# One core, hybrid decoder layer: queries and keys of the softmax heads turned in place by VectorE and stored as 128-byte pieces

## The chip, the cores and the metric

The kernel runs on one core of a Trainium2 chip. A core has TensorE (PE, matmuls; its weight loads are shown apart as PEld), VectorE (DVE), ScalarE (ACT), GpSimd (POOL) and SyncE (SP, which here issues nearly all DMAs). Every engine works off its own queue in order and waits for others through semaphores. The time is that of one execution on the device, in microseconds; less is better. It is given as the median of several runs.

## What is computed

One layer with 512 rows, width 2048, all in float32: a combined projection, gated linear attention (4 heads, "gla"), eight softmax heads of width 128 with normed queries and keys and a relative bias, an output projection, and a gated feed-forward part. For the softmax heads:

```python
h = rms_norm(x, norm1_g[l])
proj = h @ w_in[l]
qa, ka, va, ra, ga, qb, kb, vb = jnp.split(proj, split_points, axis=-1)
...
qb = rms_norm(qb.reshape(Bsz, S, DIL_HEADS, DIL_DH), q_norm_g[l])
kb = rms_norm(kb.reshape(Bsz, S, DIL_HEADS, DIL_DH), k_norm_g[l])
out_b = dilated_mixer(qb, kb, vb.reshape(Bsz, S, DIL_HEADS, DIL_DH), rel_bias)
mix = jnp.concatenate([out_a.astype(x.dtype), out_b.astype(x.dtype)], axis=-1)
x = x + mix @ w_out[l]
h2 = rms_norm(x, norm2_g[l])
x = x + (jax.nn.silu(h2 @ w_gate[l]) * (h2 @ w_up[l])) @ w_down[l]
```

In `dilated_mixer` the scores are `q · k / sqrt(128)` plus a bias; the norm weights `q_norm_g` and `k_norm_g` are vectors over the 128 features of a head, so in a score they act as a product of both, feature by feature. With 512 rows the three dilated branches reduce to a causal softmax with a bias table over the distance.

## The kernel before

**The large products** follow a scheme of seven products in place of eight (a Strassen variant). A `Pair` works on two blocks of 512 weight columns. The seven products run in the order P1, P5, P6, P3, P7, P2, P4, each over four groups of 512 rows of the weights (for the input projection). One *item* is a product with a group: its weights are a quarter (`wa`, `wb`, `wc`, `wd`, 512 KB, loaded on SP at L259) or a sum of quarters, made by DVE at L298 (P5, P6, P7 and P4 need one; P5's is `wa<-wb`). The item's weights are split in two parts for precision: `wh`, a cast on ACT (L376), and `wl`, the remainder on DVE (L380). PE then runs 8 matmuls with `wh` and 4 with `wl` (L405). There are two buffers each for `wh` and `wl`, so casts and splits run one or two items ahead of PE.

When a product closes a part of an output, ACT (L324) evicts the accumulators to `seed` tiles, DVE adds further products to them (L343), or ACT evicts into `cout` (L638, the last part); then `final` inside `final_proj` (L1072 ff.) is called with two finished tiles of 128 rows by 512 columns. For the blocks `qb0`, `kb0`, `qb1`, `kb1` (each holds four heads) `heads_norm` norms every head: squares on ACT (L1055), small steps on both engines (L178 to L183), and the scaling on DVE (L1060). Then L1086 stores the tile as rows of 2 KB to a DRAM array `proj[name]` of 512 rows by 512 columns.

**The pairs** run in this order: the gla queries and keys, `va1`/`va0`, `qb0`/`kb0`, `vb1`/`vb0`, `qb1`/`kb1`, the gate pair, two pairs of the output projection, eleven of the feed-forward part, and its down projection. A pair's last part, `cout`, is finished while the next pair begins.

**The background** is a list of generators, stepped between the items of a pair. `gla_head` pairs (L831 to L930) make the gla heads: products with constant matrices `mats` (L849, L850, L865), DVE steps L869 to L882, products L889 to L920, and squares of the result `oT` (L924), its scaling (L927) and its store (L930). `dil_heads(h)` runs two softmax heads side by side: loads of `q`, `k`, `v` and a bias tile (L959 to L963), 16 transposes on PE with 4 evictions on ACT that put the norm weight on each (L970, L971), then for blocks of 128 rows the scores (L979), logits and sums (L982 to L989), transposes of the probabilities (L996) and products with the values (L1003). Heads 0 to 3 start after `vb0` is finished, heads 4 to 7 after `qb1` is finished, beside the gate pair.

**What sets the order.** The first pair has a script; elsewhere a list scheduler lays each engine's queue from the program and its own costs. On SP each DMA also waits for the eighth DMA before it.

The lane names in the rows below: lane 0 of a head pair uses tiles `q`, `k`, `v`, `T`, `L`, `oT`; lane 1 uses `qT`, `kT`, `r`, `PT`.

Of the kernel before, what the change touches and what calls it, by code (L numbers as in the profile page):

```python
# [13 lines left out]
AF = mybir.ActivationFunctionType  # L14
ALU = mybir.AluOpType
# [3 lines left out]
P = 128  # L19
# [112 lines left out]
def block_kernel(ctx: ExitStack, tc: tile.TileContext, ins, out):  # L132
    nc = tc.nc
# [18 lines left out]
    def nm(s):  # L152
        uid[0] += 1
        return f"{s}_{uid[0]}"

    def dram(shape, name):
        return dr.tile(shape, F32, name=name, tag=name)

    def bank():
        return ps.tile([P, 512], F32, name=nm("bank"), tag="bank")  # L160

    def work(tag, shape=(P, 512), bufs=1):
        return mp.tile(list(shape), F32, name=nm(tag), tag=tag, bufs=bufs)

    def const(shape, name):
        return cp.tile(list(shape), F32, name=name, tag=name)
# [3 lines left out]
    load = nc.sync.dma_start  # L170
    store = nc.sync.dma_start

    mats = const([P, 4, P], "mats")
    ident, tri, stri, causal = (mats[:, i, :] for i in range(4))
# [95 lines left out]
    def halves(t):  # L270
        return t.rearrange("p (b a) -> p b a", b=2)
# [157 lines left out]
    def first_pair(op, rows, w1, w2, final, begin):  # L429
# [24 lines left out]
        def fetch(name, g):  # L454
            if name[0] == "r" and name != "row":
                b, h = 2 * g + (name[2] == "2"), int(name[1] == "2")
                load(raw[b, h], ins["xt"][b, h])
            elif name == "gw":
                load(kinds[:, :2].rearrange("p a g j n -> p (a g j) n"), ins["gw"])
            elif name == "sm":  # L460
                small_loads()
            else:
                q[name[0], g] = load_quarter(rows, name[0], g, w1 if name[0] in "ac" else w2)
# [169 lines left out]
    def emitted(c, scale):  # L633

        res = []
        for m in range(2):
            t = cpool.tile([P, 512], F32, name=nm("cout"), tag="C")
            nc.scalar.activation(halves(t), unfolded(c[m]), AF.Copy, scale=scale(m))  # L638
            res.append(t)
        return res  # L640
# [4 lines left out]
    gq = const([P, 1], "gq")  # L645
    gk = const([P, 1], "gk")
# [14 lines left out]
    def small_loads():  # L661
        load(mats, ins["mats"])
        load(g2, ins["g2"])
        
        load(gq, ins["q_norm_g"].rearrange("(p o) -> p o", o=1))
        load(gk, ins["k_norm_g"].rearrange("(p o) -> p o", o=1))
        nc.gpsimd.tensor_scalar(gq, gq, 1.0 / math.sqrt(128.0), None, op0=ALU.mult)
        load(gb, bass.AP(tensor=ins["gla_onorm_g"].tensor, offset=0, ap=[[0, P], [1, DV]]))

    def bias_tables():  # L670
# [49 lines left out]
    for g in range(4):  # L720
        for b in (2 * g, 2 * g + 1):
            if g < 2:
                t = apool.tile([P, 2, 512], F32, name=nm("xT"), tag="A")
# [56 lines left out]
    def gates():  # L780
# [28 lines left out]
        for t in range(4):  # L809
# [15 lines left out]
    proj = {n: dram([S, 512], n) for n in  # L825
            ("qa", "ka", "va0", "va1", "qb0", "kb0", "vb0", "vb1", "qb1", "kb1")}
# [3 lines left out]
    def head_cols(src, h, w=P):  # L830
        return src.rearrange("(t p) c -> p t c", p=P)[:, :, h * w : (h + 1) * w]  # L831
# [109 lines left out]
    def dil_head(h, lane):  # L941


        s = h // 4

        def tile_(name):
            if lane == 0:
                return work("oT" if name == "o" else name)
            if name in "qk":
                return work(name + "T")  # L950
            return rpool.tile([P, 512], F32, name=nm("r"), tag="r")

        def logits(b):
            if lane == 0:
                return work("L", bufs=2)
            return tile_("L") if b % 2 else work("PT")

        qh, kh, vh = tile_("q"), tile_("k"), tile_("v").rearrange("p (t d) -> p t d", t=4)
        load(qh.rearrange("p (t d) -> p t d", t=4), head_cols(proj[f"qb{s}"], h % 4))  # L959
        load(kh.rearrange("p (t d) -> p t d", t=4), head_cols(proj[f"kb{s}"], h % 4))  # L960
        load(vh, head_cols(proj[f"vb{s}"], h % 4))
        tb = tile_("T")
        load(tb, bass.AP(  # L963
            tensor=rep_d.tensor, offset=h * P * NB + P - 1, ap=[[NB - 1, P], [1, 512]]
        ))
        yield
        for src, g in ((qh, gq), (kh, gk)):
            tp = bank()
            for t in range(4):
                nc.tensor.transpose(tp[:, t * P : (t + 1) * P], src[:, t * P : (t + 1) * P], ident)  # L970
            nc.scalar.activation(src, tp, AF.Copy, scale=g)  # L971
        yield
        ot = tile_("o")
        lgs = {}

        def scores(b):
            n = P * (b + 1)
            lp = bank()
            nc.tensor.matmul(lp[:, :n], qh[:, b * P : (b + 1) * P], kh[:, :n], start=True, stop=True)  # L979
            lg = lgs[b] = logits(b)  # L980
            st = work("mx", (P, 4), bufs=4)
            recent["head"] = nc.vector.tensor_tensor_reduce(  # L982
                lg[:, :n], lp[:, :n], tb[:, 512 - n :], -1.0, 3.0e38, ALU.add, ALU.min, st[:, 0:1]
            ).ins
            nc.scalar.activation(
                lg[:, :n], lg[:, :n], AF.Exp, scale=-1.0, bias=st[:, 0:1], accum_out=st[:, 2:3]
            )
            nc.vector.reciprocal(st[:, 3:4], st[:, 2:3])
            recent["head"] = nc.vector.tensor_scalar(  # L989
                lg[:, :n], lg[:, :n], st[:, 3:4], None, op0=ALU.mult  # L990
            ).ins

        def turn(b, tp):
            n = P * (b + 1)
            for k in range(b + 1):
                nc.tensor.transpose(  # L996
                    tp[:, k * P : (k + 1) * P], lgs[b][:, k * P : (k + 1) * P], ident
                )
            nc.scalar.copy(lgs[b][:, :n], tp[:, :n])

        def values(b, op):
            for k in range(b + 1):
                nc.tensor.matmul(  # L1003
                    op, vh[:, k, :], lgs[b][:, k * P : (k + 1) * P], start=(k == 0), stop=(k == b)
                )

        for i in range(6):
            tp = bank() if 1 <= i <= 4 else None
            if i >= 2:
                op = tp[:, i * P : (i + 1) * P] if i < 4 else bank()[:, :P]  # L1010
                values(i - 2, op)
            if tp is not None:
                turn(i - 1, tp)
            if i >= 2:
                nc.scalar.copy(ot[:, (i - 2) * P : (i - 1) * P], op)
            if i < 4:
                scores(i)
            if i == 5:
                store(mix_d[4 + h // 2][:, :, h % 2, :].rearrange("b p n -> p b n"), halves(ot))
            yield  # L1020

    def dil_heads(h):

        lanes = [dil_head(h, 0), dil_head(h + 1, 1)]
        for _ in range(8):
            for lane in lanes:
                next(lane)
            if _ == 7:
                done.update((id(mix_d[4 + h // 2]), half) for half in range(2))
            yield  # L1030
# [17 lines left out]
    def heads_norm(tiles):  # L1048

        ss = work("ss", (P, 8), bufs=4)  # L1050
        jk = work("jk", (P, P // 2)).bitcast(mybir.dt.bfloat16)
        by_head = [t.rearrange("p (h d) -> p h d", h=4) for t in tiles]
        for m in range(2):
            for h in range(4):
                nc.scalar.activation(  # L1055
                    jk, by_head[m][:, h, :], AF.Square, accum_out=ss[:, 4 * m + h : 4 * m + h + 1]
                )
        rsqrt_mean(ss, P)
        for m in range(2):
            nc.vector.tensor_tensor(  # L1060
                by_head[m], by_head[m],
                ss[:, 4 * m : 4 * m + 4].unsqueeze(2).to_broadcast([P, 4, P]), op=ALU.mult,
            )
# [12 lines left out]
    def final_proj(n1, n2):  # L1076
        def final(half, which, tiles, acc_):
            if tiles is None:
                tiles = emitted(acc_, lambda m: row_scale(half, m))
            name = (n1, n2)[which]  # L1080
            dst = proj[name]
            if name[:2] in ("qb", "kb"):
                heads_norm(tiles)
            for m in range(2):
                r = half * 256 + m * P
                store(dst[r : r + P, :], tiles[m])  # L1086
            if half == 1 and name in ready:
                background.extend(ready[name]())

        return final  # L1090
# [521 lines left out]
```

## Time and profile before

| | |
|---|---|
| median of three runs | 1911.92 us (1911.07 to 1914.44) |
| span of the profiled execution | 1915.3 us |
| TensorE clock granted | 1.000 of full speed |
| PE busy | 1897.7 us, 99% |
| DVE busy | 1674.1 us, 87% |
| ACT busy | 1069.7 us, 56% |
| POOL busy | 12.9 us, 1% |

The profile shows one execution. Its span is from the first to the last instruction, and it is a little above the three runs that were timed. A row of the timeline reads: start, duration, engine, line, operation, output<-input, shape and count, and in brackets the idle time before it with what ended it. A row of a group gives busy time and the mean of one instruction, then the idle time of the engine just before such instructions. In a row of one source line the three durations are minimum, median and maximum in ns. TensorE takes a float32 product with one 128-row stationary operand in several passes or one, so the count in a timeline row can be twice that of the program.

### The profile page before, as it was taken

The page shows a single profiled execution, that of the slowest core. Times are in us where ns is not written, and L with a number is a line of the kernel's source. Part 1 is how long each engine was busy: PE and PEld are TensorE (multiplying, and loading weights), DVE is VectorE, ACT ScalarE, POOL GpSimd, SP SyncE. Part 2 cuts the span into 40 slices and gives each one's busy share as a digit, 9 for nine tenths or more (in the row PEclk, how much of TensorE's full clock was granted, in tenths as well). Part 3 has the DMA queues.
Part 4 walks back from the last instruction along what each step waited for, and adds up shares of the span by engine and source line. Part 5 has one row for each costly group of instructions (what it writes and reads, how often), then busy time and mean ns, then how long its engine had stood idle before and what let it go on. Part 6 is the DMA issues. An engine that isn't in the chain of part 4 may idle for free.

```text
span 1915.3 us, 25304 instructions
## 1 busy us (share of the span) xinstructions
PE 1897.7 (99%) x9002; PEld 1644.2 (86%) x9002; DVE 1674.1 (87%) x1956; ACT 1069.7 (56%) x1567; POOL 12.9 (1%) x22
## 2 busy tenths in 40 slices
PE   9999999999999999999999999999999999999999
PEld 7888888888888788888888888888888888878887
DVE  8898797778899999888888888888889979989987
ACT  8654564667776665544544544544456546536443
POOL 0000010000000000000000000000000000000000
PEclk9999999999999999999999999999999999999999
DMA  9636456444537464465465465465466675785662
GB/s 341 211 111 247 153 162 186 139 159 149 188 121 236 154 215 125 123 182 177 130 188 176 121 193 159 125 197 156 129 198 217 196 245 173 257 280 178 239 220 66
DMA packets 246806, 345.73 MB, mean 181 GB/s; under 512 B 107718, under 2 KB 154607, under 8 KB 246680
## 3 DMA queue, kind: packets, MB, share of 16 engines
q1 hardware_dynamic: 246392, 343.99, 56.5%
q8 instruction: 70, 1.15, 0.3%
q14 instruction: 56, 0.46, 0.1%
q10 hardware_dynamic: 288, 0.14, 0.0%
HBM read 286.10 MB, written 60.31 MB: 181 GB/s over the span
## 4 chain that ended last, share of the span: by engine, by line
PE 81%; DVE 5%; DMA 4%; issue 2%; ACT 1%; SPq 0%; DVEq 0%; ACTq 0%
PE acc L405 77%; DVE wl L380 2%; PE bank L1003 1%; PE bank L979 1%; DVE wa L298 1%; PE bank L996 0%; DVE AS L199 0%; DMA xn_d<-PT 0%; DMA xn_d<-oT 0%; ACT wh L376 0%; DMA wc<-in_w_down 0%; PE bank L918 0%; DMA wb<-in_w_out 0%; DMA kT<-turned_d 0%; DMA k<-y_d 0%
## 5 line engine op out<-in xcount | busy, mean ns | idle before, releaser
L405 PE MATMUL acc<-wh,AS 128*128 128x512 f32 x3008 | 711.0, 379 | 1.2 <-ACT wh L376 1.2
L405 PEld LDWEIGHTS acc<-wh,AS 128*128 128x128 f32 x3008 | 568.1, 189 | 83.0 <-ACT wh L376 2.5
L376 ACT CAST wh<-wa 128x1024 fp32r<-128x1024 f32 x376 | 394.3, 1049 | 402.4 <-PE acc L405 372.6
L405 PE MATMUL acc<-wh,AA 128*128 128x512 f32 x2256 | 533.5, 379 | 0.1
L380 DVE TENSOR_TENSOR wl<-wa,wh 128x1024 fp32r<-128x1024 f32 x376 | 456.5, 1215 | 61.3 <-ACT wh L376 49.9
L405 PEld LDWEIGHTS acc<-wh,AA 128*128 128x128 f32 x2256 | 426.1, 189 | 60.9 <-ACT wh L376 0.5
L405 PE MATMUL acc<-wl,AS 128*128 128x512 f32 x1504 | 394.0, 384 | 6.9 <-DVE wl L380 6.7
L405 PEld LDWEIGHTS acc<-wl,AS 128*128 128x128 f32 x1504 | 280.7, 189 | 56.4 <-DVE wl L380 15.8
L405 PE MATMUL acc<-wl,AA 128*128 128x512 f32 x1128 | 294.9, 384 | 0.2
L405 PEld LDWEIGHTS acc<-wl,AA 128*128 128x128 f32 x1128 | 211.2, 189 | 33.9 <-DVE wl L380 3.2
L376 ACT CAST wh<-wb 128x1024 fp32r<-128x1024 f32 x94 | 98.6, 1049 | 122.9 <-PE acc L405 113.2
L376 ACT CAST wh<-wc 128x1024 fp32r<-128x1024 f32 x94 | 98.6, 1049 | 119.3 <-PE acc L405 99.7
L376 ACT CAST wh<-wd 128x1024 fp32r<-128x1024 f32 x94 | 98.5, 1048 | 91.3 <-PE acc L405 74.0
L298 DVE TENSOR_TENSOR wa<-wc,wa 128x1024 f32<-128x1024 f32 x94 | 114.1, 1218 | 30.8 <-DMA wc<-in_w_gate 19.5
L380 DVE TENSOR_TENSOR wl<-wd,wh 128x1024 fp32r<-128x1024 f32 x94 | 114.2, 1218 | 30.2 <-ACT wh L376 26.9
L380 DVE TENSOR_TENSOR wl<-wc,wh 128x1024 fp32r<-128x1024 f32 x94 | 114.4, 1217 | 28.0 <-ACT wh L376 27.4
L380 DVE TENSOR_TENSOR wl<-wb,wh 128x1024 fp32r<-128x1024 f32 x94 | 114.2, 1215 | 9.0 <-ACT wh L376 7.3
L298 DVE TENSOR_TENSOR wb<-wd,wb 128x1024 f32<-128x1024 f32 x94 | 114.0, 1215 | 0.4
L298 DVE TENSOR_TENSOR wa<-wb,wa 128x1024 f32<-128x1024 f32 x94 | 113.6, 1210 | 0.8
L298 DVE TENSOR_TENSOR wa<-wd,wa 128x1024 f32<-128x1024 f32 x94 | 112.9, 1215 | 0.1
L343 DVE SCALAR_TENSOR_TENSOR seed<-acc,rs,seed 128x512 f32<-128x512 f32 x96 | 70.3, 744 | 15.3 <-PE acc L405 14.1
L324 ACT ACTIVATE seed<-acc,rs 128x512 f32<-128x512 f32 x96 | 60.7, 681 | 5.1 <-PE acc L405 5.1
(317 smaller groups left out, 1263.0 us busy)
## 6 DMA issues: line engine op xcount, KB each, us to landing
wa<-in_w_gate SPq DMA_DIRECT2D x44, 512.0 KB, 3.4
wb<-in_w_up SPq DMA_DIRECT2D x44, 512.0 KB, 5.8
wd<-in_w_up SPq DMA_DIRECT2D x44, 512.0 KB, 4.2
wc<-in_w_gate SPq DMA_DIRECT2D x44, 512.0 KB, 3.4
wa<-in_w_in SPq DMA_DIRECT2D x24, 512.0 KB, 5.1
wc<-in_w_in SPq DMA_DIRECT2D x24, 512.0 KB, 3.6
wb<-in_w_in SPq DMA_DIRECT2D x24, 512.0 KB, 5.4
wd<-in_w_in SPq DMA_DIRECT2D x24, 512.0 KB, 5.1
```

Source lines behind the costliest of these rows:

```text
L298: nc.vector.tensor_tensor(src, other, src, op=ALU.subtract)
L324: nc.scalar.activation(halves(t), unfolded(src[m]), AF.Copy, scale=self.scale(half, m))
L343: nc.vector.scalar_tensor_tensor(halves(seed[m]), unfolded(src[m]), self.scale(half, m), halves(seed[m]), op0=ALU.mult, op1=ALU.add,)
L376: nc.scalar.copy(high[k], sources[k])
L380: recent["low"] = nc.vector.tensor_tensor(low[k], sources.pop(k), high[k].bitcast(F32), op=ALU.subtract).ins
L405: nc.tensor.matmul(p.dst[prod][m], a[:, jj, hl, m * P : (m + 1) * P], folded(w[i][:, jj, :]), start=fresh and g == 0 and i == 0 and jj == ...
L979: nc.tensor.matmul(lp[:, :n], qh[:, b * P : (b + 1) * P], kh[:, :n], start=True, stop=True)
L1003: nc.tensor.matmul(op, vh[:, k, :], lgs[b][:, k * P : (k + 1) * P], start=(k == 0), stop=(k == b))
```

## The change

Four things change, and the rest of the program is the same text.

1. Each finished tile of `qb*` and `kb*` (128 rows, 512 columns) is transposed in place by DVE. That operation turns each block of 32 by 32 by itself: partition `32a + i`, column `32c + n` receives what stood in partition `32a + n`, column `32c + i`.
2. The turned tile is stored by four DMAs, one for each 32 partitions: each writes 32 × 16 pieces of 32 numbers (128 bytes), so that `proj[name]` now holds features as rows and tokens as columns. There are 64 such stores of 64 KB in place of 16 of 256 KB.
3. The loads of `q` and `k` for a head become 128 whole rows of 2 KB, already turned. The 16 transposes of each head pair on PE (64 in all) go, as do their 16 evictions on ACT.
4. The norm weight of the queries, already divided by sqrt(128), is multiplied once with that of the keys on POOL. One ACT operation per head puts this product on the queries (8 in all); the keys are used as loaded.

```diff
@@ small_loads
         nc.gpsimd.tensor_scalar(gq, gq, 1.0 / math.sqrt(128.0), None, op0=ALU.mult)
+        nc.gpsimd.tensor_tensor(gq, gq, gk, op=ALU.mult)
@@ dil_head
-        load(qh.rearrange("p (t d) -> p t d", t=4), head_cols(proj[f"qb{s}"], h % 4))
-        load(kh.rearrange("p (t d) -> p t d", t=4), head_cols(proj[f"kb{s}"], h % 4))
+        load(qh, proj[f"qb{s}"][h % 4 * P : h % 4 * P + P, :])
+        load(kh, proj[f"kb{s}"][h % 4 * P : h % 4 * P + P, :])
...
-        for src, g in ((qh, gq), (kh, gk)):
-            tp = bank()
-            for t in range(4):
-                nc.tensor.transpose(tp[:, t * P : (t + 1) * P], src[:, t * P : (t + 1) * P], ident)
-            nc.scalar.activation(src, tp, AF.Copy, scale=g)
+        nc.scalar.activation(qh, qh, AF.Copy, scale=gq)
@@ final_proj
-            if name[:2] in ("qb", "kb"):
+            turned = name[:2] in ("qb", "kb")
+            if turned:
                 heads_norm(tiles)
             for m in range(2):
                 r = half * 256 + m * P
-                store(dst[r : r + P, :], tiles[m])
+                if not turned:
+                    store(dst[r : r + P, :], tiles[m])
+                    continue
+                nc.vector.transpose(tiles[m], tiles[m])
+                for a in range(4):
+                    store(
+                        dst.rearrange("(c i) t -> i c t", i=32)[:, :, r + 32 * a : r + 32 * a + 32],
+                        tiles[m][32 * a : 32 * a + 32, :].rearrange("i (c n) -> i c n", n=32),
+                    )
```

In the changed program the lines behind these edits have other numbers: the scaling of the heads is L1057 (before L1060), the transposes L1087, the stores L1089 (before L1086), the scale of the queries L968, the scores L976 (before L979), the transposes of the probabilities L993 (before L996) and the products with the values L1000 (before L1003); the lines of gla are one higher.

The scheduler orders the queues anew. The first place is the start of the pair `vb1`/`vb0`, while `qb0`'s last part, `cout`, is finished. On DVE before, the sums for P5 (`wa<-wb`) stand between the splits; this piece holds those of its second and third group (`wa_2537`, `wa_2577`), and the scaling of `cout` (L1060) follows five rows on:

```order
L298 TENSOR_TENSOR wa_2537<-wb_2668,wa_2537 128x1024
L380 TENSOR_TENSOR wl_2622<-wa_2577,wh_2618 128x1024
L181 SCALAR_TENSOR_TENSOR so_2550<-so_2550,rt_2558 128x2
L298 TENSOR_TENSOR wb_2668<-wd_2785,wb_2668 128x1024
L182 TENSOR_TENSOR so_2550<-so_2550,rt_2558 128x2
L298 TENSOR_TENSOR wa_2577<-wb_2705,wa_2577 128x1024
L183 SCALAR_TENSOR_TENSOR so_2550<-so_2550,rt_2558 128x2
L178 TENSOR_SCALAR ss_2593<-ss_2593 128x8
L380 TENSOR_TENSOR wl_2652<-wa_2620,wh_2647 128x1024
```

On DVE at this place now (`cout_2614` and `cout_2616` are the two tiles, `oT_2576` the gla result, and `wa_2562<-wb_2701` is the sum of P5's second group):

```order
L928 SCALAR_TENSOR_TENSOR oT_2576<-bank_2574,so_2575,gb 128x256 x2
L1057 TENSOR_TENSOR cout_2614<-cout_2614,ss_2618 128x512
L1057 TENSOR_TENSOR cout_2616<-cout_2616,ss_2618 128x512
L1087 STREAM_TRANSPOSE cout_2614<-cout_2614 128x512
L1087 STREAM_TRANSPOSE cout_2616<-cout_2616 128x512
L870 SCALAR_TENSOR_TENSOR qT_2784<-bank_2774,L_2721 128x4x64
L298 TENSOR_TENSOR wa_2562<-wb_2701,wa_2562 128x1024
```

The sum that P5's second group needs has moved behind the scaling and the transposes of `cout`, and behind a gla step.

On PE at the same place before, P5's second group (`wh_2703`, `wl_2708`) runs around the gla products L865, and its third (`wh_2724`) follows at once:

```order
L405 MATMUL acc_2701<-wh_2703,AS_77_529 128x512 x2
L405 MATMUL acc_2702<-wh_2703,AS_77_529 128x512 x2
L865 MATMUL bank_2741<-mats,q_2637 128x128 x4
L865 MATMUL bank_2742<-mats,k_2639 128x128 x4
L405 MATMUL acc_2701<-wl_2708,AS_77_529 128x512
L405 MATMUL acc_2702<-wl_2708,AS_77_529 128x512
L405 MATMUL acc_2701<-wl_2708,AS_77_529 128x512
L405 MATMUL acc_2702<-wl_2708,AS_77_529 128x512
L405 MATMUL acc_2701<-wh_2724,AS_81_549 128x512 x2
```

On PE now, from the end of P5's second group (`wl_2741`) to its third (`wh_2757`):

```order
L405 MATMUL acc_2735<-wl_2741,AS_77_530 128x512
L890 MATMUL bank_2833<-qT_2784,kT_2788 64x128
L890 MATMUL bank_2833<-L_2721,kT_2788 64x128
...
L902 MATMUL bank_2846<-v_2674,k_2672 128x256 x2
L919 MATMUL bank_2895<-v_2674,PT_2831 128x256 x2
L921 MATMUL bank_2895<-st_2849,qT_2784 128x256
L405 MATMUL acc_2734<-wh_2757,AS_81_550 128x512 x2
```

The whole gla step, to its result `bank_2895`, now stands between two items. On DVE and ACT that result's squares, scaling and the sum for `wh_2757` follow it in this order: on DVE `L928 ... oT_2897`, then `L298 ... wa_2602`, whose cast is `wh_2757`.

The second place is the start of the gate pair, where heads 4 and 5 begin. On PE before, their transposes stand within the last P5 item (`wh_4337`, `wl_4342`), and the next item follows:

```order
L405 MATMUL acc_4278<-wh_4337,AS_56_388 128x512 x2
L970 MATMUL bank_4371<-mats,q_4296 128x128 x4
L970 MATMUL bank_4377<-mats,k_4297 128x128 x4
L970 MATMUL bank_4383<-mats,qT_4304 128x128 x4
L970 MATMUL bank_4389<-mats,kT_4305 128x128 x4
L405 MATMUL acc_4277<-wl_4342,AS_56_388 128x512
```

On PE now, from the end of P5's third group (`wl_4342`) to its fourth (`wh_4358`):

```order
L405 MATMUL acc_4299<-wl_4342,AS_81_550 128x512
L976 MATMUL bank_4437<-k_4318,q_4317 128x128
L976 MATMUL bank_4446<-kT_4326,qT_4325 128x128
L993 MATMUL bank_4476<-mats,L_4439 128x128
L976 MATMUL bank_4479<-k_4318,q_4317 128x256
L993 MATMUL bank_4487<-mats,PT_4448 128x128
L976 MATMUL bank_4490<-kT_4326,qT_4325 128x256
L1000 MATMUL bank_4514<-L_4439,v_4319 128x128
L976 MATMUL bank_4520<-k_4318,q_4317 128x384
L1000 MATMUL bank_4528<-PT_4448,r_4327 128x128
L976 MATMUL bank_4534<-kT_4326,qT_4325 128x384
L405 MATMUL acc_4298<-wh_4358,AS_56_389 128x512 x2
```

Ten products of the heads stand in a row between two items, where before the first scores came two items after the transposes. On SP, at the same place, the eight stores of `cout` stand directly ahead of the loads of `k`, `v`, the bias and `q`. On DVE the sum for `wh_4358` stands behind the first two rounds of both heads:

```order
L985 RECIPROCAL mx_4449<-mx_4449 128x1
L986 TENSOR_SCALAR PT_4448<-PT_4448,mx_4449 128x128
L298 TENSOR_TENSOR wa_4244<-wb_4339,wa_4244 128x1024
L985 RECIPROCAL mx_4482<-mx_4482 128x1
L979 ISA r_4492,mx_4493<-bank_4490,r_4331 128x256
```

Before, that sum (`wa<-wb` of the fourth group) came before the heads' first scores.

## The prediction

> **What bounds the kernel now.** I read the page from the top (busy shares, then the chain that ended last) and then what TensorE waits for.
>
> ```profile
> span 1915.3 us, 25304 instructions
> PE 1897.7 (99%) x9002; PEld 1644.2 (86%) x9002; DVE 1674.1 (87%) x1956; ACT 1069.7 (56%) x1567; POOL 12.9 (1%) x22
> PE 81%; DVE 5%; DMA 4%; issue 2%; ACT 1%; SPq 0%; DVEq 0%; ACTq 0%
> L405 PE MATMUL acc<-wl,AS 128*128 128x512 f32 x1504 | 394.0, 384 | 6.9 <-DVE wl L380 6.7
> ```
>
> PE is busy for 99% of the span and its largest wait, for the split `wl`, is 6.7 us in all. So a PE instruction that goes is worth its time, and a new wait of PE costs its length unless matmuls stand in front of it. VectorE at 87% is close behind, and in the stretch where the change hits first it is full:
>
> ```profile
> 258.00:292.00 34.00, 34.00 (x176) 29.29 (x175) 33.42 (x55) 20.60 (x51) 8.05 (x3) 1.00 0.35 109
> ```
>
> The columns after the stretch's length are PE, weight loads, DVE, ACT and POOL busy: DVE 33.42 of 34.00 us.
>
> **What goes from PE.** The chain of waits holds the removed transposes (L970) as whole pieces; three of the four:
>
> ```profile
> 334.23 1.75 PE bank L970 x16
> 388.39 1.75 PE bank L970 x16
> 463.45 1.75 PE bank L970 x16
> ```
>
> Sixteen take 1.75 us, and there are four groups (64 fewer matmuls on PE): 4 × 1.75 = **−7.0 us**. The Trainium skill, VectorE: DVE Perf Modes, section The three transpose paths, has 390 ns for one 128x128 transpose on TensorE (bf16): by that the removal would be worth 64 × 0.39 = 25.0 us, an estimate from that page, and the whole change would save about 6. The trace differs, as 1.75 / 16 is 0.109 us in a pipelined row, so its value stands.
>
> **What is added off PE.** Sixteen in-place DVE transposes; no such instruction is in the trace in place, but the same shape between two tiles is:
>
> ```profile
> L1396 DVE STREAM_TRANSPOSE oT<-seed x22: 700/704/711, 770.7 to 1511.0; 128x512 f32<-128x512 f32 x22
> L1086 SPq DMA_DIRECT2D qb<-cout x4: 319/320/320, 278.4 to 456.9; - x4
> DMA to landing us min/median/max: 2.0/2.3/5.8
> L1398 SPq DMA_DIRECT2D turned_d<-PT x88: 302/504/1530, 775.1 to 1518.3; - x88
> L1398 SPq DMA_DIRECT2D turned_d<-oT x88: 302/488/1785, 771.5 to 1513.2; - x88
> DMA to landing us min/median/max: 1.7/2.2/5.0
> ```
>
> I take 0.70 us each, 11.2 in all; 0.68 and the 1.23 of a 1024-wide operation bound it. Twelve of the sixteen I cost at nothing: they stand beside long rows of matmuls whose sums are ahead. Without that cover the same twelve would cost 8.4. The stores go from 16 of 2 KB rows to 64 of 512 pieces of 128 bytes. The nearest rows are L1398's, 64 KB also in many short pieces: 0.49 us to issue, 2.2 to land, against 0.32 and 2.3 of a row store (L1086). So four stores hold SP for 1.96 us instead of 0.32. The loads of q and k become contiguous; the strided ones land in 3.5 (below), and between 2.1 and 5.0, the fastest and slowest loads of that size, I keep 3.5. ACT loses 16 evictions of about 0.68 us and gains 8 scales that I price the same: 5.4 us less work on an engine that is not the bound. The one product on POOL, at the start, is hidden by 12.9 us busy in 1915.
>
> **Place A, the start of the pair after qb0/kb0 (264 to 290 us).** In the order of the change, ACT's cast for P5's second group and the DVE sum before it stand behind the whole finishing of `cout`, and the gla steps are bunched on PE. Rows of before that price it:
>
> ```profile
> 276.87 1.26 ACT L324 ACTIVATE seed<-acc,rs 128x512 f32<-128x512 f32 x2
> 265.45 0.39 ACT L924 ACTIVATE oT<-bank 128x256 f32<-128x256 f32 x1 [0.17 <-DMA ong_d<-oT]
> 266.08 0.20 ACT L924 ACTIVATION_READ_ACCUMULATOR oT<-bank 128x1 f32 x1
> 259.04 0.17 DVE L178 TENSOR_SCALAR ss<-ss 128x8 f32<-128x8 f32 x1
> 260.32 1.29 DVE L1060 TENSOR_TENSOR seed<-seed,ss 128x512 f32<-128x512 f32 x2
> 261.54 0.87 DVE L927 SCALAR_TENSOR_TENSOR oT<-bank,so,gb 128x256 f32<-128x256 f32 x2
> 283.38 0.41 DVE L869 SCALAR_TENSOR_TENSOR qT<-bank,L 128x256 f32<-128x256 f32 x1
> 263.57 1.23 DVE L298 TENSOR_TENSOR wa<-wb,wa 128x1024 f32<-128x1024 f32 x1
> 262.22 1.05 ACT L376 CAST wh<-wa 128x1024 fp32r<-128x1024 f32 x1 [1.49 <-PE acc L405]
> 274.10 1.05 PE L849 MATMUL bank<-mats,T 128*128 128x128 f32 x8
> 275.45 1.43 PE L405 MATMUL acc<-wl,AA 128*128 128x512 f32 x4
> 276.72 1.89 PE L405 MATMUL acc<-wh,AS 128*128 128x512 f32 x8
> 279.31 1.89 PE L405 MATMUL acc<-wh,AS 128*128 128x512 f32 x8
> 281.04 0.60 PE L865 MATMUL bank<-mats,q 128*128 128x128 f32 x4
> 281.83 1.11 PE L405 MATMUL acc<-wl,AS 128*128 128x512 f32 x4
> ```
>
> From the end of P1 on PE: evictions 1.26; squares of `oT` 0.83 (265.45 to 266.28); the norm's small steps 1.28 (259.04 to 260.32); `cout` scaled and `oT` written 2.09 (260.32 to 262.41); two transposes 1.40; L869 0.41; the sum 1.23; the cast 1.05. That is 9.55, with 0.3 for handovers 9.85. In front of P5's second group PE has one item (276.72 to 279.31, 2.59), the eight-and-two small ones (274.10 to 275.45, 1.35) and L865 (281.04 to 281.83, 0.8): 4.75. PE waits 9.85 − 4.75 = **5.1**.
>
> Then P5's third group: PE runs the gla outputs (L921 of the change) and has nothing after them until squares 0.83, small steps 1.28, `oT` 0.87, sum 1.23, cast 1.05 and 0.3 of handovers are done: **5.6**. Place A costs 10.7. In before the same sums stood between the splits, one or two items early, and no row above shows PE idle.
>
> The loads behind the eight stores on SP:
>
> ```profile
> wb<-in_w_in SPq DMA_DIRECT2D x24, 512.0 KB, 5.4
> ```
>
> P1 ends at 275.45 + 1.43 = 276.88, both tiles are turned 6.86 later at 283.7 (the five terms up to the transposes), the first at 283.0; eight issues of 0.49 end at 287, and `wb` lands at 292.8. The sum that reads it comes at 276.88 + 9.85 + 2.59 (an item) + 2.2 (gla products, an estimate) + 2.98 (squares, steps, `oT`) = 294.5. So SP hides it by 1.7 us; if the issues took 0.7 it would not. At the kb groups too SP is held 3.3 us longer (8 × 0.49 − 2 × 0.32) ahead of weight loads that are issued several items early; I price this at nothing, at most 3.3 a group.
>
> **Place B, the gate pair's first heads (453 to 480 us).** The change lays the scores of heads 4 and 5 on PE straight behind P5's third group and ahead of its fourth, whose sum is also behind two rounds of the heads on DVE. Rows:
>
> ```profile
> 454.39 1.22 DVE L298 TENSOR_TENSOR wa<-wd,wa 128x1024 f32<-128x1024 f32 x1
> 455.52 1.28 DVE L1060 TENSOR_TENSOR cout<-cout,ss 128x512 f32<-128x512 f32 x2
> q<-qb SPq DMA_DIRECT2D x4, 256.0 KB, 3.5
> 464.45 0.68 ACT L971 ACTIVATE q<-bank,gq 128x512 f32<-128x512 f32 x1
> 458.97 1.89 PE L405 MATMUL acc<-wh,AS 128*128 128x512 f32 x8
> 461.56 1.89 PE L405 MATMUL acc<-wh,AS 128*128 128x512 f32 x8
> 470.21 0.38 PE L979 MATMUL bank<-k,q 128*128 128x128 f32 x2
> 470.44 0.39 PE L979 MATMUL bank<-kT,qT 128*128 128x128 f32 x2
> 473.33 0.28 DVE L989 TENSOR_SCALAR PT<-PT,mx 128x128 f32<-128x128 f32 x1
> ```
>
> The sum at 454.39 that stood ahead of L1060 stands earlier now, so the norm can start at 454.4 and the first tile is turned by 454.4 + 1.28 + 0.70 = 456.4. Eight stores of 0.49 end at 460.3, the last lands 2.2 later at 462.5, q's load (0.4 to issue, 3.5 to land) at 466.4, the scale ends 0.68 later: 467.1. The third group ends at 461.56, 0.3 later as its neighbour's split waits for the transposes: 461.9. PE waits **5.2**, and 0.3 more for the split. From the first scores to the second head's scaled logits before took 3.4 (470.21 to 473.61); then sum 1.22, cast 1.05, 0.3: 6.0. In that time PE has ten small products: scores of 128, 256 and 384 columns for two heads at 0.23 a 128 columns (470.21 to 470.44), 2 × 6 × 0.23 = 2.8, and four of 128 columns at half that or more, 0.5: an estimate of 3.3, so it waits **2.7**. Place B costs 8.2.
>
> **Sum:** −7.0 + 10.7 + 8.2 = +11.9. The profiled span would go from 1915.3 to 1927; that execution is just above the three runs (1911.07 to 1914.44), so I carry the difference to their median 1911.92 and forecast **1924 us**. From 560 us on the two orders agree; between 500 and 560 some rows change places, for which I allow 2 us either way.
>
> **The rivals.**
> 1. *The covers hold* (faster). If PE's queue reaches both places late enough, or the handovers are shorter, that the sums come in time, only the removal is left: 1911.9 − 7.0 = 1904.9. It needs PE to be over 10 us behind ACT at the two places; ACT's evictions wait for the end of PE's own P1, which speaks against it. It decides only where place A and B together cost under 3. Chance 0.07.
> 2. *One place waits*: with A alone 1911.9 − 7.0 + 10.7 = 1915.6, with B alone 1913.1. For it: B's first half falls to 3.8 if q lands in 2.1. Against it: both waits are made by the order of a queue, which no duration undoes. Chance 0.12.
> 3. *The short pieces are slow.* If each store of place B took 1.785 to issue and 5.0 to land, the worst of L1398, q would come 8 × 1.30 + 2.8 = 13 us later: 1937. For it: pieces of 128 bytes, 512 of them in 64 KB; against it: medians of 0.49 and 2.2. Chance 0.14. The Trainium skill, DMA: Bandwidth & Descriptors, section Specifications, wants at least 512 bytes per transfer for line rate and says that below it data is read, modified and written; that speaks for this rival, and L1398's median shows none of it, but its landing is of 64 KB only.
>
> My forecast has 0.67, with a range of its own of 1916 to 1932: unknown prices (in-place transpose 0.68 to 1.23, load 2.1 to 5.0, the region after 500) move it by some 8 either way. The range of 8 in 10 takes in one-place cases and the lower half of the slow stores: 1912 to 1935. A measurement tells about 0.2%, 3.8 us: under 1908.1 is faster (rival 1, 0.07), within it are the one-place cases and a little of the forecast's edge (0.12), above 1915.7 the rest, 0.81.
>
> **What would show it.** L970 gone and PE's matmuls 64 fewer; a wait of L405 for ACT's `wh` of about 5 us twice near 275 to 290; PE's scores (L976 of the change) waiting for ACT's q near 462, then L405 for `wh` again; store issues of L1089 at 0.5 us. If these waits are under 1 us each I am wrong about the order deciding; if the stores take over 1 us to issue, rival 3 holds; if waits stand past 560 us, something I did not see moved.

## The result and the profile after

| | before | changed |
|---|---|---|
| median of the timed runs | 1913.18 us (1911.07 to 1917.69, 4 runs) | 1935.86 us (1934.73 to 1936.59, 4 runs) |
| span of the profiled execution | 1915.3 us | 1934.8 us |
| clock granted to PE, mean | 1.000 | 0.993 |

The ratio is 1.0116 with a 95% interval of 1.0105 to 1.0128; the medians lie 22.7 us apart. The forecast was 1924 us with a range up to 1935, so the direction was right, the forecast loss was about half of the measured one, and the time lies 0.9 us outside the range.

The head of the page of the changed kernel, and its list of what PE waited for (total, times, longest):

```profile
span 1934.8 us, 25201 instructions
PE 1902.5 (98%) x8938; PEld 1645.0 (85%) x8938; DVE 1684.0 (87%) x1972; ACT 1066.5 (55%) x1559; POOL 6.7 (0%) x23
...
PE acc L405 <- ACT wh L376: 9.3, 2, 5.4
PE bank L976 <- ACT q L968: 5.3, 1, 5.3
PE acc L405 <- DVE wl L380: 4.8, 9, 0.9
PE bank L993 <- DVE L L986: 2.0, 2, 1.5
PE bank L1105 <- DVE seed L1153: 2.0, 1, 2.0
```

The reader is to see that PE is *busier* than before (1902.5 against 1897.7 us) with 64 matmuls fewer, although the waits that were forecast are there too. Both waits for the cast `wh` stand at place A, that for the scaled `q` at place B. That matmuls took longer shows in the clock that PE was granted. These are stretches of the changed kernel (the columns behind the length are the busy times of PE, weight loads, DVE, ACT and POOL, then PE's clock, the busy share of the DMA engines and GB/s); before, the clock was 1.00 in all four:

```profile
280.00:300.00 20.00, 10.71 (x49) 7.62 (x48) 13.33 (x28) 5.14 (x12) 1.25 (x2) 0.77 0.73 229
300.00:320.00 20.00, 20.00 (x83) 17.18 (x84) 17.60 (x16) 9.12 (x14) 0.00 (x0) 0.89 0.15 49
460.00:480.00 20.00, 14.65 (x67) 12.21 (x66) 10.41 (x15) 7.80 (x18) 0.00 (x0) 0.96 0.44 117
480.00:500.00 20.00, 18.41 (x70) 14.36 (x71) 15.85 (x31) 11.19 (x22) 0.00 (x0) 0.78 0.59 227
```

And PE's own rows at place A (start, duration):

```profile
278.28 1.03 PE L405 MATMUL acc<-wl,AS 128*128 128x512 f32 x4
...
285.72 3.78 PE L405 MATMUL acc<-wh,AS 128*128 128x512 f32 x8 [3.92 <-ACT wh L376]
289.29 1.80 PE L405 MATMUL acc<-wl,AS 128*128 128x512 f32 x4
...
299.84 0.80 PE L405 MATMUL acc<-wh,AS 128*128 128x512 f32 x1 [5.37 <-ACT wh L376]
```

Eight products with `wh` that took 1.89 us before take 3.78: behind each wait PE ran at half clock, and the item after the first wait lasted 5.3 us (285.72 to 291.02) instead of 2.6. (The last row is the first matmul of its item; all eight took 3.78 us here too.)

At place B the chain runs along SP, and the first scores, which took 0.38 us before, take 0.80:

```profile
468.99 4.17 SPq L1089 DMA_DIRECT2D qb<-cout  x8
474.92 0.33 SPq L960 DMA_DIRECT2D q<-qb  x1
478.97 0.72 ACT L968 ACTIVATE q<-q,gq 128x512 f32<-128x512 f32 x1 [9.80 <-DMA q<-qb]
479.74 0.80 PE L976 MATMUL bank<-k,q 128*128 128x128 f32 x2 [5.34 <-ACT q L968]
478.60:488.80 10.20, 7.47 (x19) 4.80 (x20) 6.22 (x17) 5.99 (x14) 0.00 (x0) 0.50 1.04 399
```

The load of `q` stands behind the eight stores and lands 4.0 us after its issue. The last row is a stretch: for these 10.2 us the clock was 0.50, and PE was busy for 7.5 of them.

**Where the time came from.** PE runs the same 659 items (P1 to P4 of all pairs but the first) in the same sequence in all kernels here, so the start of an item can be compared. The table gives how much later it starts than in the first profile of before:

| kernel (profile) | item 54 (258 us before) | 66 (297) | 95 (387) | 128 (498) | 147 (566) | last (1910) |
|---|---|---|---|---|---|---|
| the change | 0.8 | 16.1 | 14.3 | 21.9 | 24.8 | 19.5 |
| e6, before again | 1.4 | 1.4 | 1.4 | 1.4 | 1.0 | -1.4 |
| e1, row stores | 0.4 | 0.4 | -1.3 | -3.5 | -1.9 | -7.2 |
| e2, pieces only | 1.3 | 12.6 | 10.9 | 19.9 | 22.3 | 16.8 |
| e3, waits filled | 1.0 | 11.5 | 11.7 | 19.1 | 21.2 | 16.3 |
| e5, SP and ACT | 2.5 | 2.5 | 3.9 | 3.1 | 5.5 | 0.8 |
| e7, bare removal | 0.1 | 0.1 | -1.7 | -3.5 | -0.7 | -3.3 |
| e9, bare, heads 0 to 3 | 1.7 | 1.7 | 1.0 | -0.8 | 0.0 | -4.8 |
| e10, bare, heads 4 to 7 | 0.0 | 0.0 | 0.0 | -0.3 | 5.0 | 0.4 |
| e11, heads 0 to 3, SP and ACT | 0.7 | 0.7 | 0.3 | -1.5 | -1.1 | -6.8 |
| e12, heads 0 to 3, SP | 0.4 | 16.1 | 14.9 | 13.1 | 15.0 | 10.1 |
| e13, heads 4 to 7, SP | 0.3 | 0.3 | 0.3 | 9.4 | 9.6 | 3.9 |
| e14, e12 with its waits filled | -0.3 | 10.2 | 12.8 | 12.1 | 11.8 | 6.3 |

For the change: place A costs 16.1 − 0.8 = 15.3 us, the two groups of transposes at 334 and 388 us bring 1.8 each (item 128 is behind both), place B costs 21.9 − (16.1 − 3.5) + 1.75 = 11.1 with the third group, and between 498 and 566 us another 2.9 + 1.75 = 4.7 come although the fourth group is gone. Behind 566 us the first profile of before is itself slow by some waits that its second profile has less of (−2.4 there), so the last column is read with 2 to 3 us of doubt, and the times decide.

### The profile page after: what moved, and what is told of

Read it like the earlier page. It is cut to its first block, busy times and chain, and to the rows that moved or that the text cites. A ratio compares the mean times of both kernels' runs of the same rounds, so it can differ in the third digit from the quotient of the medians.

```text
span 1934.8 us, 25201 instructions
## 1 busy us (share of the span) xinstructions
PE 1902.5 (98%) x8938; PEld 1645.0 (85%) x8938; DVE 1684.0 (87%) x1972; ACT 1066.5 (55%) x1559; POOL 6.7 (0%) x23
## 4 chain that ended last, share of the span: by engine, by line
PE 81%; DVE 6%; DMA 3%; issue 2%; ACT 1%; SPq 0%; DVEq 0%; ACTq 0%
PE acc L405 76%; DVE wl L380 2%; DVE wa L298 1%; PE bank L1000 1%; PE bank L976 1%; DVE AS L199 1%; DMA top<-mix_d 0%; PE bank L993 0%; PE bank L1105 0%; ACT wh L376 0%; DMA mix_d<-r 0%; PE bank L919 0%; DMA qT<-S_d 0%; DMA wc<-in_w_down 0%; PE bank L902 0%
## 5 line engine op out<-in xcount | busy, mean ns | idle before, releaser
L405 PEld LDWEIGHTS acc<-wh,AS 128*128 128x128 f32 x3008 | 570.4, 190 | 92.7 <-ACT wh L376 11.1
L298 DVE TENSOR_TENSOR wa<-wc,wa 128x1024 f32<-128x1024 f32 x94 | 114.5, 1221 | 30.9 <-DMA wc<-in_w_gate 20.5
L298 DVE TENSOR_TENSOR wb<-wd,wb 128x1024 f32<-128x1024 f32 x94 | 114.1, 1218 | 0.4
L298 DVE TENSOR_TENSOR wa<-wb,wa 128x1024 f32<-128x1024 f32 x94 | 113.5, 1210 | 0.8
L298 DVE TENSOR_TENSOR wa<-wd,wa 128x1024 f32<-128x1024 f32 x94 | 112.9, 1216 | 0.1
L343 DVE SCALAR_TENSOR_TENSOR seed<-acc,rs,seed 128x512 f32<-128x512 f32 x96 | 70.3, 744 | 14.3 <-PE acc L405 14.2
```

The source lines that it names most:

```text
L298: nc.vector.tensor_tensor(src, other, src, op=ALU.subtract)
L343: nc.vector.scalar_tensor_tensor(halves(seed[m]), unfolded(src[m]), self.scale(half, m), halves(seed[m]), op0=ALU.mult, op1=ALU.add,)
L405: nc.tensor.matmul(p.dst[prod][m], a[:, jj, hl, m * P : (m + 1) * P], folded(w[i][:, jj, :]), start=fresh and g == 0 and i == 0 and jj == ...
```

## The experiments

In all of them the median of before was 1912.3 to 1913.8 us, run beside them on the same chip. Where the heads read a wrong arrangement, the expectation says so.

**e1 and e2: the stores or the transposes?** e1 keeps VectorE's transposes and stores rows; e2 keeps the pieces and drops the transposes.

```diff
 e1
-                for a in range(4):
-                    store(dst.rearrange(...)[...], tiles[m][32 * a : 32 * a + 32, :]...)
+                store(dst[r : r + P, :], tiles[m])
 e2
-                nc.vector.transpose(tiles[m], tiles[m])
```

> The change, but each turned tile is stored by one DMA of 2 KB rows in place of four of 128-byte pieces (the heads then read queries and keys in a wrong arrangement, the work of every engine but the DMA pieces is that of the change). Theory, that the loss is the queue order which the many small stores brought about, and the halved clock behind the waits: the queues stand as before at both places, so only the 64 transposes go from PE: about 1913 - 7 = 1906 us, no PE wait over 2 us, clock 1.000. Rival, that VectorE's 16 transposes in a full stretch make the sums late: above 1920, with waits of PE for the cast at 280 to 300 us as in the change.

Measured: 1910.29 us, ratio 0.9984 (0.9975 to 0.9994), clock 1.0.

> The change without the 16 transposes on VectorE (blocks are stored unturned, so the heads read other numbers), with the 64 stores of 128-byte pieces. Theory: the stores bring the order, so it stays slow: 1925 to 1940, with one or two waits of PE of over 4 us near 280 to 300 us and half clock behind each. Rival, that the transposes on VectorE cost the time: about 1906, as PE has lost its transposes and VectorE has gained none.

Measured: 1932.13 us, ratio 1.0097 (1.0082 to 1.0112). What PE waited for, first e1, then e2:

```profile
PE acc L405 <- DVE wl L380: 5.6, 8, 1.9
PE bank L993 <- DVE L L986: 3.1, 2, 2.3
```

```profile
PE acc L405 <- ACT wh L376: 12.0, 3, 6.1
PE acc L405 <- DVE wl L380: 4.4, 6, 1.5
PE bank L993 <- DVE L L986: 4.1, 2, 2.2
```

The waits for the cast come with the pieces on SP and go with them; VectorE's 16 transposes alone make none. In e1 PE's queue at both places is that of before, in e2 the gla steps are bunched too. So the loss hangs on the 64 small stores on SP and the queue order that comes with them. At place A the chain to the late cast holds no DMA, so there it is the order; at place B the eight issues on SP are themselves in the chain, and e1 shortens them as well as it changes the order, so the two are not told apart there. And e1 saved 2.5 us, not the 7 of its expectation.

**e3: fill the waits at place A.** Ten products into a bank that nobody reads: four behind L866 and, in the piece below, six behind L921 of that head.

```diff
+            if h == 3 and ts == (0, 1):
+                wb_ = bank()
+                for _ in range(6):
+                    with tc.issue_after(last):
+                        nc.tensor.matmul(wb_, ident, mats.rearrange("p a n -> p (a n)"), start=True, stop=True)
```

> The change with ten products of no use laid on PE inside the two waits at 282 and 295 us (four of 0.86 us and six, into a bank that nobody reads); all other queues in the same order. Theory, that the waits cost once as idle time and once more as half clock behind them: the idle time stays, filled, and the half clock goes: 5.1/2 + 4.7/2 = 4.9 us less than the change, about 1931, and the granted clock after 284 and 298 us is 1.0. Rival, that the half clock costs nothing because PE waits for others then anyway: within 1 us of the change, 1935 to 1937.

Measured: 1936.08 us, ratio 1.0117 (1.0102 to 1.0132): no gain in the times. In its profile the clock behind the waits was full,

```profile
286.00:288.00 2.00, 2.00 (x10) 1.76 (x11) 1.78 (x3) 0.00 (x0) 0.00 (x0) 1.00 0.70 120
300.00:302.00 2.00, 2.00 (x11) 1.75 (x10) 2.00 (x2) 0.89 (x1) 0.00 (x0) 1.00 0.02 9
```

and the item behind them started 4.6 us earlier than in the change, but PE then waited 1.7 us for a cast at 321 us. Inconclusive as to the time; e12 and e14 repeat it with place A alone.

**e4 and e5: the whole change, its stores on other queues.** In e4 POOL issues those of `kb0`, `kb1` and `qb0`, and SP and ACT in turn those of `qb1`; in e5 SP and ACT in turn issue all.

```diff
 e4
+                    q = nc.gpsimd if name != "qb1" else (nc.sync, nc.scalar)[a % 2]
 e5
+                    q = (nc.sync, nc.scalar)[a % 2]
-                    store(
+                    q.dma_start(
```

> The whole change, but the stores of kb0, kb1 and qb0 are issued by POOL and those of qb1 by SP and ACT in turn; with this PE's queue stands as before at both places. Theory: 1913 - 7 = 1906 us, up to 1909 if ACT's four issues of about 0.5 us delay a cast; clock 1.000. Rival, that pieces of 128 bytes themselves are too slow for the heads' loads or for the weight loads beside them: 1916 or more, with PE waiting for the scale of q or for a weight sum.

Measured: 1955.65 us, ratio 1.0222 (1.0205 to 1.0239). Far slower, and by neither mechanism. POOL's timeline:

```profile
289.50 0.66 POOL L1090 DMA_DIRECT2D qb<-seed  x1 [1.80 <-issue]
291.96 0.65 POOL L1090 DMA_DIRECT2D qb<-seed  x1 [1.80 <-issue]
294.41 0.66 POOL L1090 DMA_DIRECT2D qb<-seed  x1 [1.80 <-issue]
```

POOL put out one such store every 2.45 us, against 0.50 on SP, so eight took 20 us; gla's small steps on POOL stood behind them (PE waited 11.1 us for one), and later the loads of `k` and what SP held behind those (15.6 us for a cast).

> The whole change, but the stores of 128-byte pieces are issued by SP and ACT in turn, half each, and none by POOL. PE's queue stands nearly as before at the first place, and at the second the heads' scores stand some four items later than in the change. Theory: no PE wait over 3 us at either place, clock 1.000, so that only the shorter PE work and the later stretch count: like the row stores, 1909 to 1913 us, at most 4 more from ACT's 32 issues of 0.54. Rival, that the pieces themselves are too slow: above 1920 with a wait for the scale of q of over 4 us.

Measured: 1914.75 us, ratio 1.0013 (1.0004 to 1.0022), clock 1.0; the longest waits of PE were

```profile
PE acc L405 <- DVE wl L380: 8.8, 12, 1.7
PE bank L1106 <- DVE seed L1154: 2.6, 1, 2.6
```

This is the whole change, with all its pieces and transposes, 21 us faster than as it was written: neither the pieces nor the transposes are slow. Why it gains nothing over before is not shown; by the table it is 2.5 us late before place A and loses 2.4 + 1.75 us between items 128 and 147, and its ACT issues were not tried apart.

**e6: before again.** Nothing is changed.

> The kernel before, unchanged, for a second profiled execution. If the waits of PE between 630 and 1700 us (7.7 us in the first profile: 1.16 at 634, 0.84 at 719, 1.18 at 1691, 1.54 at 1695 and others) differ from run to run, they are smaller here and the span nearer 1911; if they belong to the kernel, they stand again and the later queues of the change would be better by some 4 us.

Measured: a span of 1913.8 us in that one execution, and 2.4 us less behind 566 us than in the first profile. Waits of 0.6 to 2.8 us stood at other places and in other sizes: so they belong to the execution, as far as these two show, and not to the kernel.

**e7, e9 and e10: the removal by itself.** No transposes on VectorE, row stores; for all heads (e7), for heads 0 to 3 alone (e9), for heads 4 to 7 alone (e10).

```diff
 e9 (e10: s == 1)
+        if s == 0:
             nc.scalar.activation(qh, qh, AF.Copy, scale=gqk)
+        else:
+            for src, g in ((qh, gq), (kh, gk)):
+                ...
```

> Only the removal: no transposes on PE, none on VectorE, stores as rows of 2 KB (the heads then read queries and keys in a wrong arrangement). PE's queue is that of the row stores nearly everywhere. If the part of the 7.0 us that did not show with row stores (2.5 were seen) was eaten by VectorE's 16 transposes of 0.69, this is faster than row stores by up to 4.5: 1906. If it was eaten by the order of the heads' steps between 500 and 560 us, which is the same here, it is as with row stores, 1909 to 1911, and PE waits again for VectorE near 500 us.

Measured: 1910.5 us, ratio 0.9985 (0.9976 to 0.9994): like the row stores.

> The bare removal (no transposes on PE or VectorE, 2 KB rows stored) for heads 0 to 3 alone, whose products stand between 330 and 400 us; heads 4 to 7 as before (heads 0 to 3 read queries and keys in a wrong arrangement). PE's queue is that of before but for 32 transposes. Theory, that the 7.0 us are given back only beside the gate pair (509 to 566 us): the two groups here keep their worth, 1912.3 - 3.5 = 1908.8, and the time between items 131 and 147 is that of before. Rival, that any saving is given back there, because something off PE sets the end of that stretch: 1911 to 1913, with 3 us more of waits of PE between 500 and 560 us.

Measured: 1910.17 us, ratio 0.9984 (0.9975 to 0.9992), 3.0 us faster.

> The bare removal for heads 4 to 7 alone, whose products stand beside the gate pair, heads 0 to 3 as before (heads 4 to 7 read queries and keys in a wrong arrangement). Theory, that the new order of the heads' steps there (two rounds in one item) gives back 4 to 6 us: -3.5 + 4 to 6 = 1913 to 1915, no gain, with PE waiting for VectorE at the first transposes of the probabilities near 505 us. Rival, that the give-back follows PE's lead of 7 us and not the order: with half the lead about half is lost, 1911.

Measured: 1914.33 us, ratio 1.0002 (0.9993 to 1.0010): no gain. PE's waits in e10 and its rows where it lost the lead (line 1005 is the transposes of the probabilities there):

```profile
PE bank L1005 <- DVE L L998: 2.8, 2, 2.0
PE bank L1112 <- DVE seed L1160: 2.3, 1, 2.3
```

```profile
507.94 0.29 DVE L998 TENSOR_SCALAR L<-L,mx 128x128 f32<-128x128 f32 x1
...
508.29 0.33 PE L1005 MATMUL bank<-mats,L 128*128 128x128 f32 x1 [2.01 <-DVE L L998]
```

Half of the removal keeps its worth (3.5 expected, 3.0 measured), and the half beside the gate pair is worth nothing: there PE waits for the softmax steps on VectorE, whose rounds stand two in one item now. In e10 the clock also fell to half behind both waits shown (for 3.41 us from 509.8 and from 547.3 us); in e1, with waits of 2.3 and 1.1 us at these places, it did not.

**e8: what a wait costs.** The kernel before with ten waits of 5 to 17 us in ten feed-forward pairs, far from anything else.

```diff
+            if k in WAITS:
...
+                nc.tensor.transpose(bk[:, :P], ident, ident)
...
+                nc.vector.tensor_copy(t, bk[:, :64])
+                for _ in range(WAITS[k]):
+                    nc.gpsimd.tensor_scalar(t, t, 1.0, None, op0=ALU.mult)
...
+                recent["held"] = nc.tensor.transpose(bk[:64, P : 2 * P], t, ident).ins
```

> The kernel before with ten waits of different length put on PE, one in each of ten feed-forward pairs (PE turns a tile, POOL works on it 2, 4, 6, 8, 10, 12, 14, 18, 22 and 28 times, PE turns it back and only then goes on). Theory: short waits cost their length and leave the clock at 1.0; from some length between 2 and 4 us on the granted clock falls to 0.5 for 3.4 or 6.8 us, so that such a wait costs its length and about 1.7 to 3.4 us more. Rival: the clock falls with the share of idle time over a longer stretch, so that single waits of any of these lengths leave it at 1.0.

Measured: 2034.82 us in one execution, mean clock 0.975. POOL was slower than planned, so no wait was short and the threshold was not found here. The shortest:

```profile
818.41 0.27 PE L410 MATMUL bank<-mats 128*128 128x128 f32 x1
823.73 0.42 PE L416 MATMUL bank<-mats,hold 128*64 128x128 f32 x1 [5.05 <-POOL hold L414]
823.81 3.41 PE L421 MATMUL acc<-wh,AS 128*128 128x512 f32 x8
827.05 1.03 PE L421 MATMUL acc<-wl,AS 128*128 128x512 f32 x4
```

Between 824 and 827 us the clock was 0.55. All ten waits were followed by half clock. An item 14 places on was later by the wait, by the 0.35 us of the two inserted products, and by 1.5 to 3.0 us more, 2.2 in the mean, and nothing of it had come back there.

**e11: a version that may beat both.** The change for heads 0 to 3 alone, with one of each four stores on ACT and the others on SP.

```diff
+                if not turned or name[2] != "0":
...
+                    q = nc.scalar if a == 3 else nc.sync
```

> The change in full, but for heads 0 to 3 alone: VectorE's transposes, stores of 128-byte pieces, three of each four on SP and one on ACT, the product of both norm weights on the queries; heads 4 to 7 as before. PE's queue stands as before at the first place. Theory: -3.5 for the transposes of PE, up to +3 for ACT's eight issues and the fuller VectorE before 290 us: 1909 to 1912, faster than both kernels or equal to before. Rival, that 32 pieced stores alone make waits at 245 to 290 us: above 1913.

Measured: 1910.6 us, ratio 0.9987 (0.9978 to 0.9995): 2.5 us under before, and 25 under the change. The head of its page and its longest waits of PE:

```profile
span 1908.6 us, 25254 instructions
PE 1893.1 (99%) x8970; PEld 1643.9 (86%) x8970; DVE 1677.7 (88%) x1964; ACT 1067.7 (56%) x1563; POOL 6.0 (0%) x23
...
PE acc L405 <- DVE wl L380: 4.9, 6, 1.0
PE bank L1118 <- DVE seed L1166: 1.4, 1, 1.4
```

**e12 to e14: each place by itself.** The change for heads 0 to 3 alone (place A), for heads 4 to 7 alone (place B), all stores on SP; and e12 with its waits filled as in e3.

> The change in full for heads 0 to 3 alone, all its stores on SP; heads 4 to 7 as before. PE's queue is that of the change at the first place and that of before from there on, so this times place A by itself. By the profile of the change, place A costs 15.3 us and the removal there brings 3.5: 1912.7 + 11.8 = 1924.5. If waits cost only their length (9.3), 1912.7 + 9.3 - 3.5 = 1918.5.

Measured: 1926.09 us, ratio 1.0061 (1.0047 to 1.0075): 12.3 us by the medians, as the profile's 15.3 − 3.5.

> The change in full for heads 4 to 7 alone, all its stores on SP; heads 0 to 3 as before. PE's queue is that of before at the first place and that of the change from the second on. By the profile of the change: place B 11.1, removal -3.5, given back beside the gate pair 4.7: 1912.7 + 12.3 = 1925. If waits cost only their length (6.9) and the removal kept its worth: 1916. The two kernels together should give the 22.7 of the change if nothing else is in it.

Measured: 1921.09 us, ratio 1.0040 (1.0028 to 1.0052): 7.3 us by the medians, less than the 12.3 of the profile's sum and more than waits alone. In its profile place B cost as much as in the change, but only 0.2 + 1.75 us came between 498 and 566 us.

> As the kernel of place A alone, with four and six products of no use (0.86 us each) on PE inside its two waits, all else in the same order. If the half clock behind the waits sets the time there, it is 4 to 5 us faster than the kernel of place A without them, about 1920. If VectorE, which is full behind the waits, sets it, the two are within 1.5 us of each other.

Measured: 1922.74 us, ratio 1.0044 (1.0032 to 1.0056): 3.4 us under e12 by the medians; the two intervals overlap a little. In the profile it was 5.9 us ahead of e12 at item 66 and 2.1 at item 95, as PE then waited 2.4 us for a cast whose sum waited for a weight load:

```profile
313.74 0.33 SPq L259 DMA_DIRECT2D wc<-in_w_in  x1
...
319.38 1.22 DVE L298 TENSOR_TENSOR wa<-wc,wa 128x1024 f32<-128x1024 f32 x1 [3.81 <-DMA wc<-in_w_in]
...
321.79 2.60 PE L405 MATMUL acc<-wh,AS 128*128 128x512 f32 x8 [2.39 <-ACT wh L376]
```

The same load was issued at 301.21 us before: SP is 12.5 us later with it, PE only 10.2 later at item 66. So neither the half clock alone nor a full VectorE: behind place A SP's queue is late too, and some of what the clock gives back is lost there.

## Why the prediction came out too small

**What was right.** That the queues decide, and where: both waits of place A and that of place B are there, and their lengths are near the forecast ones (3.92 and 5.37 us for 5.1 and 5.6; 5.34 for 5.2). The prices, by the rows of the changed kernel:

```profile
L1087 DVE STREAM_TRANSPOSE seed<-seed 128x512 f32<-128x512 f32 x12 | 7.8, 686 | 0.0
...
L1089 SPq DMA_DIRECT2D qb<-cout x16: 303/508/515, 282.6 to 472.6; - x16
DMA to landing us min/median/max: 1.7/1.9/1.9
...
L968 ACT ACTIVATE q<-q,gq x4: 712/721/723, 322.2 to 508.4; 128x512 f32<-128x512 f32 x4
```

A transpose took 0.69 us (0.70 was taken), a store 0.51 to issue and 1.9 to land (0.49 and 2.2), the scale 0.72 (0.68), the load of `q` 4.0 (3.5). The prediction's lower bound of 2.1 us for that load was misread: 2.1 is the landing of stores (`qb<-cout`); the loads of queries and keys took 2.8 to 5.0 before. The slow pieces of rival 3 did not come about. Its number, 1937, is near the time for another reason, which is luck. The rule of the Trainium skill that it cites (DMA: Bandwidth & Descriptors, section Specifications: at least 512 bytes for line rate) shows in none of these rows as a longer landing. Of the signs named, the second wait of place B did not come for the cast: PE waited 0.6 and 0.9 us for the softmax steps instead. And a wait of 2.0 us stood at 567 us, past the 560 us from which the prediction expected none.

**The step that failed is the sum.** It put each wait in at its own length and nothing for what follows it, and it counted the removal in full. So one term was missing and one was too large.

1. *What follows a wait.* Place A was put at 10.7 us, its waits were 9.3, and it cost 15.3; place B was put at 8.2, its waits were 5.3 and 1.5, and it cost 11.1. The items behind place A's waits ran 5.3 and 5.0 us instead of 2.6, together 5.1 more. At place B PE was busy for 7.5 us at half clock; at full clock that work would have taken half, 3.7 less (an estimate), and 5.3 + 1.5 + 3.7 = 10.5 of the 11.1. e8 shows the same in a quiet stretch: 2.2 us for each wait, on top of its length. With some 2.2 us for each of its four waits the forecast would have come to about 1933. How much of this reaches the end of the kernel is less sure: full clock at place A was worth 3.4 us of the time by the medians in e14, not all 5.1, and in e3, with place B behind it, nothing that the times show. The Trainium skill, TensorE: Matmul & The Clock Gate, section Part 1, says that PE falls to half clock after about 3.4 us of idling and needs about as long a busy window to come back. That rule speaks against this change, and the prediction did not weigh it. The runs agree with it in the pieces of half clock, 3.41 us and multiples, but not in the idling: in the change the clock fell 2.2 us into the wait of 3.92, and a wait of 1.95 us was followed by half clock too.

2. *The removal was counted in full.* −7.0 holds on PE at the places themselves (1.75 for each group, in every kernel), but beside the gate pair 4.7 us came back in the change (3.4 to 7.0 in e1, e7 and e10). The prediction allowed 2 us there. PE waited 1.5 and 2.0 us there for VectorE, against 0.5 and 1.1 before, and ran at half clock behind the second wait; e1 lost least, without half clock, and e10 most, with two pieces of it. e9 and e10 show that the groups at 334 and 388 us keep their worth and the two later ones have none.

With these terms the change's profile adds up: −7.0 + 15.3 + 11.1 + 4.7 = 24.1; with the start (+0.8) and the end (−5.3, the slow end of before's first profile among it) that is 19.6, and the spans differ by 19.5. By the times it is 22.7, since the first profile of before lay above its median; carrying a span's difference over to a median was right only within some 3 us. Timed one by one, place A and place B sum to 19.6 us, with intervals that reach 22.7 when taken together.

**What stays open.** Why the scheduler lays the queues so when SP has many small stores is argued, not shown: by e1 and e2 the order hangs on them, but its own reckoning was not looked at. Place B's waits were not filled, so what its half clock costs the time is known from the profile alone, and why e3 shows no gain where e14 does is open. The 3 us by the medians between the sum of the two places and the whole were not tried apart; in the profiles the two add up at item 147 (15.0 + 9.6 against 24.8).

## What to carry to other kernels

An order that a scheduler makes can turn on a detail that costs nothing on the chip: read the new order first, and where it lays a chain bare, price the wait, the slow clock behind it and the queue that falls behind. Shortening the busiest engine pays only where it is the bound in that stretch; the same 1.75 us were worth their length beside the gla and value pairs and nothing beside the gate pair. Here many small stores did best spread over two queues (e5, e11), and worst on an engine whose issues are slow (POOL in e4).

## What the runs showed of the hardware

- Every wait of PE of 2.8 us and more in these traces was followed by half clock, in pieces of 3.41, 6.83 and 10.24 us and longer (17.07 at the wait of 15.6 us in e4). In the change half clock set in while PE still waited, 2.2 us into the wait of 3.92 and 4.2 into that of 5.34. Between 1.8 and 2.6 us it was not uniform: after a wait of 1.95 us in the change, and after 2.01 and 2.31 in e10, the clock fell for 3.41 us; after 2.31 us in e1 and 2.61 in e5 it did not. Waits of up to 1.5 us never brought it down.
- POOL put out a store of 512 pieces of 128 bytes every 2.45 us, SP every 0.50.
- A 64 KB store in pieces of 128 bytes landed in 1.9 us, a 256 KB store in rows of 2 KB in 2.3.
